# Gated linear attention: the short levels' differences kept, their products computed in one burst

## The chip, the cores and the metric

The kernel runs on one NeuronCore of one Trainium2 chip. The metric is the device time of one execution in microseconds (us), as the median of several runs; lower is better. The engines are called as the profile calls them: PE (TensorE), DVE (VectorE), ACT (ScalarE), POOL (GpSimd) and SP (SyncE, which issues most of the transfers).

## What is computed

One layer of a hybrid decoder, for a prompt of 512 tokens and 8 sample tokens. One combined projection feeds a dilated window attention and a gated linear attention (GLA) of 4 heads; then come an output merge, a projection and a feed-forward part. The change lies in the prompt's GLA alone, which the reference computes chunk by chunk:

```python
cum = jnp.cumsum(gc, axis=2)
diff = cum[:, :, :, None, :] - cum[:, :, None, :, :]
decay = jnp.exp(jnp.where(causal[None, None, :, :, None], diff, -jnp.inf))
scores = jnp.einsum('bhtsd,bhsd->bhts', qc[:, :, :, None, :] * decay, kc)
o = (jnp.einsum('bhts,bhsv->bhtv', scores, vc)
     + jnp.einsum('bhtd,bhdv->bhtv', qc * jnp.exp(cum), state))
```

So for each pair of tokens s <= t of a chunk the score is the sum over 128 features of q(t) k(s) exp(cum(t) - cum(s)).

## The kernel before, in words

The kernel holds activations with features on the 128 partitions and 520 tokens (512 of the prompt, 8 samples, in two halves of 260) along the free dimension. Every projection is a chain of panels: 128 output columns of a weight, loaded by SP, split by ACT (`whi`, L90) and DVE (`wlo`, L91) into two parts, and multiplied on PE in three passes by the halves of the activations (`panel_mms`, L124). A panel has 48 such matmuls of 128x260; the text calls them panel matmuls.

The attention and GLA parts are written as Python generators. `fill` advances one of them between panels, so that their small instructions are recorded among the panel matmuls. What is recorded is not yet the order: the framework's scheduler (a timeline model in the build) then orders each engine's instructions, within the dependencies, the priorities (`split_panel` has a high one) and the buffers of the pools.

GLA takes one head after another (`gla`), in chunks of 128 tokens, while the projections of the GLA inputs and of the two output gates (`gA`, `gB`) run. For one head: `zp` (the gate's matmul), its log-sigmoid on ACT and DVE, the running sum `cum` (L567), the operands `qe` and `kl` (multiplied on POOL, L574 and L579), and the transposes `klp` on PE (L582). Then come the scores, by levels. A pair of tokens whose common block has length 2L (first in the left half, second in the right half) belongs to level L; with a difference `D` of `cum` to the value at the middle of the block, the left half of `D` becomes k exp(-D/16) and the right half q exp(D/16), and one product gives all pairs of the level. LEVELS is (64, 32, 16, 8, 4, 2). Each level has one DVE subtraction (L609), two exponentials on ACT (L611, L612), two multiplications on DVE (L613, L614) and matmuls into a PSUM bank `lev`. Level 64 takes 4 matmuls of 64x64 (L617) and level 32 takes 8 of 32x32 (L622); DVE copies them into the score tile `ST` (L618, L626). The four short levels (16, 8, 4, 2) use `blocks` (L552): 16 matmuls, each of a 32-token block with itself, each into one quarter of the partitions. DVE merges each of them into `sd` under the mask of the level (`copy_predicated`, L630). Ahead of the levels stands a group for a token with itself and for neighbouring pairs (two calls of `blocks`, L601 and L602 merge them). POOL copies `sd` into `ST` (L633), and `ST` is an operand of the outputs `gpo` (L639).

Most matmuls use the array at its full width of 128 columns; `blocks`, level 32 and the sample's `gso` use 32 columns, level 64 uses 64. The text calls them narrow, and a stretch of narrow matmuls without a wide one between them a run.

Of the kernel before, what the change touches and what calls it, by code (L numbers as in the profile page):

```python
# [9 lines left out]
F32 = mybir.dt.float32  # L10
F32R = mybir.dt.float32r
U8 = mybir.dt.uint8
AF = mybir.ActivationFunctionType
ALU = mybir.AluOpType
# [3 lines left out]

D = 1024
S = 512  # L20
NB = 8
P = 128
# [5 lines left out]
LEVELS = (64, 32, 16, 8, 4, 2)  # L28
# [16 lines left out]
class Build:  # L45
# [175 lines left out]
    def stats(self, ap, xr):  # L221
# [14 lines left out]
        for j in range(2):  # L236
            self.rsqrt(ap, self.rb[:, j * HC:(j + 1) * HC], pr[:, j, :HC], HC, 1 / D)

# [316 lines left out]
    def gla(self, gp, h):  # L555
        nc = self.nc
        k, q = self.QKb[:, h, :S], self.QKb[:, 4 + h, :S]
# [2 lines left out]
        zp = self.bank("zp")  # L560
        nc.tensor.matmul(zp, wg, pv(halves(self.G)), start=True, stop=True)
        cum = gp.tile([P, S], F32, tag="cum", name="cum", bufs=1)
        D = gp.tile([P, S], F32, tag="D", name="D", bufs=3)
        self.logsig(gp, D, zp, S)
        for c in range(4):
            cc = slice(c * P, (c + 1) * P)
            nc.vector.tensor_tensor_scan(cum[:, cc], self.ones, D[:, cc], 0.0, op0=ALU.mult, op1=ALU.add)  # L567
        yield
# [8 lines left out]
                                op=ALU.subtract)  # L577
# [9 lines left out]
        sd = gp.tile([P, 4, 32], F32, tag="sd", name="sd", bufs=1)  # L587
# [3 lines left out]
        lm = lambda n: self.c["lmask"][:, n].unsqueeze(1).to_broadcast([P, 4, 32])  # L591

        vw = lambda t, L: t.rearrange("p (n x l) -> p n x l", x=2, l=L)
        D = gp.tile([P, S], F32, tag="D", name="D", bufs=3)[:, :256]
        nc.vector.tensor_tensor(D, cum[:, 1::2], cum[:, 0::2], op=ALU.subtract)
        nc.scalar.activation(D, D, AF.Exp, scale=1 / 16)
        nc.vector.tensor_tensor(D, D, q[:, 1::2], op=ALU.mult)
        ps = self.bank("lev")[:, :192].rearrange("p (c t) -> p c t", c=4)
        self.blocks(ps[:, :, :32], k, q, 32)
        self.blocks(ps[:, :, 32:], k, D, 16)  # L600
        nc.vector.copy_predicated(sd, lm(0), ps[:, :, :32])  # L601
        nc.vector.copy_predicated(sd[:, :, 1::2], lm(1)[:, :, 1::2], ps[:, :, 32:])  # L602
        yield
        for li, L in enumerate(LEVELS):
            ps = self.bank("lev")
            n = S // (2 * L)
            D = gp.tile([P, S], F32, tag="D", name="D", bufs=3)
            Dv, kv, qv = (vw(t, L) for t in (D, k, q))
            nc.vector.tensor_tensor(D.rearrange("p (n l) -> p n l", n=n), cum.rearrange("p (n l) -> p n l", n=n),  # L609
                                    vw(cum, L)[:, :, 0, L - 1:L].to_broadcast([P, n, 2 * L]), op=ALU.subtract)  # L610
            nc.scalar.activation(Dv[:, :, 0], Dv[:, :, 0], AF.Exp, scale=-1 / 16)  # L611
            nc.scalar.activation(Dv[:, :, 1], Dv[:, :, 1], AF.Exp, scale=1 / 16)  # L612
            nc.vector.tensor_tensor(Dv[:, :, 0], Dv[:, :, 0], kv[:, :, 0], op=ALU.mult)  # L613
            nc.vector.tensor_tensor(Dv[:, :, 1], Dv[:, :, 1], qv[:, :, 1], op=ALU.mult)  # L614
            if L == 64:
                for c in range(4):
                    nc.tensor.matmul(ps[:64, c * 64:(c + 1) * 64], Dv[:, c, 0], Dv[:, c, 1], start=True, stop=True)  # L617
                nc.vector.tensor_copy(ST[:64, :, 64:], ps[:64, :256].rearrange("p (c t) -> p c t", c=4))  # L618
            elif L == 32:
                for c in range(4):  # L620
                    for x in range(0, P, 64):
                        nc.tensor.matmul(ps[x:x + 32, c * 32:(c + 1) * 32], Dv[:, 2 * c + x // 64, 0],  # L622
                                         Dv[:, 2 * c + x // 64, 1], start=True, stop=True)
                for x in range(0, P, 64):
                    rows = slice(x, x + 32)
                    nc.vector.tensor_copy(ST[rows, :, x + 32:x + 64], ps[rows, :P].rearrange("p (c t) -> p c t", c=4))  # L626
            else:
                psv = ps[:, :P].rearrange("p (c t) -> p c t", c=4)
                self.blocks(psv, D, D, 32)
                nc.vector.copy_predicated(sd, lm(li), psv)  # L630
            yield
        for x in range(0, P, 32):
            nc.gpsimd.tensor_copy(ST[x:x + 32, :, x:x + 32], sd[x:x + 32])  # L633
        st = None
# [2 lines left out]
        for c in range(4):  # L637
            po = self.bank("gpo")
            nc.tensor.matmul(po[:, :256], ST[:, c], V[:, c], start=True, stop=(c == 0))  # L639
            if c:  # L640
                nc.tensor.matmul(po[:, :256], qe[:, c * P:(c + 1) * P], st, start=False, stop=True)  # L641
            pu = self.bank("gpu")
            nc.tensor.matmul(pu[:, :256], klT[:, c * P:(c + 1) * P], V[:, c], start=True, stop=True)  # L643
            sn = gp.tile([P, 256], F32, tag="state", name="state", bufs=2)
            if c:
                nc.vector.scalar_tensor_tensor(sn, st, el[:, c:c + 1], pu[:, :256], op0=ALU.mult, op1=ALU.add)
            else:
                nc.vector.tensor_copy(sn, pu[:, :256])
            st = sn
            nc.scalar.activation(os[:, c], po[:, :256], AF.Copy)  # L650
            jk = gp.tile([P, S], F32, tag="D", name="jk", bufs=3)
            nc.scalar.activation(jk[:, :256], po[:, :256], AF.Square, accum_out=ssq[:, c:c + 1])
            yield
        nc.gpsimd.dma_start(self.O["pgla"][h], st)
# [494 lines left out]
```

## Time and profile before

| what | value |
|---|---|
| median of 3 runs | 945.26 us (945.14 to 946.29) |
| the profiled execution | 943.87 us |
| its span, first to last instruction | 942.1 us |
| mean granted TensorE clock | 0.993 |

The profile is one execution. The time around its span is 1.8 us, and the execution lies 1.4 us under the median. In a row of the timeline stand the start, the busy time, the engine, the line, the operation with output and inputs, the size and a count; a bracket at the end tells how long the engine had been idle and what ended that. Starts of consecutive matmuls, not their busy times, tell what a matmul costs, since matmuls are pipelined. An fp32 matmul leaves two records, one of a panel or a transpose leaves one; so 16 matmuls of `blocks` are 32 records.

### The profile page before, as it was taken

The numbers are of one execution on the slowest core, as the hardware profiler recorded it, in microseconds if no ns is written. First come the engines' busy times: TensorE is split into PE (matmuls) and PEld (weight loads), VectorE is DVE, ScalarE is ACT, GpSimd is POOL, SyncE is SP. The second block draws the span as 40 slices with busy tenths as digits, with TensorE's granted clock in tenths as the row PEclk, the third lists the DMA queues.
The fourth block names the chain that finished last, engine by engine and source line by source line (L and its number), as shares of the span: only waits on it lengthen the run. The fifth ranks groups of instructions, "written<-read, shape, count | busy, mean of one in ns | idle before, by whom it ended". The sixth has DMA issues, their size and how long they took to land.

```text
span 942.1 us, 19815 instructions
## 1 busy us (share of the span) xinstructions
PE 921.9 (98%) x8290; PEld 902.7 (96%) x8290; DVE 550.0 (58%) x1079; ACT 376.7 (40%) x732; POOL 72.4 (8%) x125
## 2 busy tenths in 40 slices
PE   6999999999999999999999999999999999999995
PEld 6999999999988998999999999999999999999995
DVE  6756746844775958676755556433443344555664
ACT  5232233362544545564733444422432243224432
POOL 4000001000201112010000000000000000000000
PEclk9999999998999999999999999999999999999998
DMA  6366545311545344222677766777775222323301
GB/s 226 126 219 223 187 145 204 113 68 47 160 165 200 114 163 143 83 73 70 230 269 268 269 246 247 269 275 275 276 270 179 90 91 89 100 102 98 128 25 67
DMA packets 37579, 155.27 MB, mean 165 GB/s; under 512 B 5177, under 2 KB 11585, under 8 KB 35538
## 3 DMA queue, kind: packets, MB, share of 16 engines
q1 hardware_dynamic: 32498, 95.26, 29.6%
q0 software_dynamic: 4848, 58.73, 17.9%
q8 instruction: 65, 1.06, 0.5%
q14 instruction: 24, 0.20, 0.1%
q10 hardware_dynamic: 144, 0.01, 0.0%
HBM read 140.66 MB, written 54.17 MB: 207 GB/s over the span
## 4 chain that ended last, share of the span: by engine, by line
PE 96%; DVE 2%; issue 1%; ACT 1%; DMA 0%; SPq 0%; DVEq 0%; ACTq 0%
PE mps L124 80%; PE mps L981 5%; PE pvp L365 1%; PE lev L552 1%; PE ptp L354 1%; PE gpo L639 1%; PE gpu L643 1%; PE vps L305 1%; PE gso L706 1%; PE gpo L641 1%; PE spO L151 1%; PE sps L339 1%; DMA raw<-in_w_in 0%; PE mps L516 0%; PE sps L334 0%
## 5 line engine op out<-in xcount | busy, mean ns | idle before, releaser
L90 ACT ACTIVATE whi<-raw 128x512 fp32r<-128x512 f32 x264 | 165.8, 630 | 372.6 <-PE mps L124 329.8
L91 DVE TENSOR_TENSOR wlo<-raw,whi 128x512 fp32r<-128x512 f32 x264 | 182.4, 692 | 148.3 <-ACT whi L90 145.9
L124 PE MATMUL mps<-uh,whi 128*128 128x260 f32 x928 | 195.3, 290 | 6.6 <-ACT whi L90 5.3
L124 PE MATMUL mps<-ul,whi 128*128 128x260 f32 x928 | 194.5, 289 | 1.9 <-DVE ul L215 1.9
L124 PE MATMUL mps<-uh,wlo 128*128 128x260 f32 x928 | 193.8, 288 | 0.0
L124 PEld LDWEIGHTS mps<-uh,whi 128*128 128x128 f32 x928 | 145.8, 191 | 9.4 <-ACT whi L90 6.4
L124 PEld LDWEIGHTS mps<-ul,whi 128*128 128x128 f32 x928 | 145.6, 191 | 5.1 <-DVE ul L215 2.5
L124 PEld LDWEIGHTS mps<-uh,wlo 128*128 128x128 f32 x928 | 146.3, 191 | 1.3 <-issue 0.6
L124 PE MATMUL mps<-hh,whi 128*128 128x260 f32 x512 | 103.2, 283 | 0.0
L124 PE MATMUL mps<-hh,wlo 128*128 128x260 f32 x512 | 103.2, 283 | 0.0
L124 PE MATMUL mps<-hl,whi 128*128 128x260 f32 x512 | 103.0, 283 | 0.0
L124 PEld LDWEIGHTS mps<-hh,whi 128*128 128x128 f32 x512 | 79.0, 188 | 0.1
L124 PEld LDWEIGHTS mps<-hh,wlo 128*128 128x128 f32 x512 | 78.9, 188 | 0.0
L124 PEld LDWEIGHTS mps<-hl,whi 128*128 128x128 f32 x512 | 78.7, 188 | 0.0
L124 PE MATMUL mps<-fh,wlo 128*128 128x260 f32 x384 | 77.3, 283 | 0.0
L124 PE MATMUL mps<-fl,whi 128*128 128x260 f32 x384 | 77.2, 283 | 0.0
L124 PE MATMUL mps<-fh,whi 128*128 128x260 f32 x384 | 76.8, 282 | 0.0
L124 PEld LDWEIGHTS mps<-fh,wlo 128*128 128x128 f32 x384 | 59.2, 188 | 0.0
L124 PEld LDWEIGHTS mps<-fl,whi 128*128 128x128 f32 x384 | 59.0, 188 | 0.0
L124 PEld LDWEIGHTS mps<-fh,whi 128*128 128x128 f32 x384 | 59.0, 188 | 0.0
L981 PE MATMUL mps<-fh,lw 128*128 128x260 f32 x256 | 46.6, 283 | 0.0
L981 PEld LDWEIGHTS mps<-fh,lw 128*128 128x128 f32 x256 | 39.6, 188 | 0.1
(334 smaller groups left out, 1312.8 us busy)
## 6 DMA issues: line engine op xcount, KB each, us to landing
raw<-in_w_in SPq DMA_DIRECT2D x57, 512.0 KB, 3.5
raw<-in_w_up SPq DMA_DIRECT2D x32, 512.0 KB, 4.8
raw<-in_w_down SPq DMA_DIRECT2D x32, 512.0 KB, 4.8
sx<-in_state SPq DMA_DIRECT2D x8, 512.0 KB, 4.3
sx<-dV SPq DMA_DIRECT2D x8, 512.0 KB, 4.7
out_sgla<-sx POOLq DMA_DIRECT2D x8, 512.0 KB, 5.4
raw<-in_w_pb SPq DMA_DIRECT2D x8, 512.0 KB, 5.8
raw<-in_w_o SPq DMA_DIRECT2D x8, 512.0 KB, 5.7
```

Source lines behind the costliest of these rows:

```text
L90: nc.scalar.activation(hi, raw[:, x:x + n], AF.Copy)
L91: nc.vector.tensor_tensor(lo, raw[:, x:x + n], hi.bitcast(F32), op=ALU.subtract)
L124: self.last = nc.tensor.matmul(out[j], w, x[:, k, j * HC:(j + 1) * HC], start=(k == 0 and n == 0), stop=(k == kt - 1 and n == 2))
L151: self.nc.tensor.matmul(*args, **kw)
L305: nc.tensor.transpose(pt[:, r * P:(r + 1) * P], vt[:, r * P:(r + 1) * P], self.c["ident"])
L339: nc.tensor.matmul(pss[hh][:, hp, gg * P:(gg + 1) * P], Q[rows, i, b * P:(b + 1) * P], K[rows, i, b * P:(b + 1) * P], start=True, stop=True)
L354: nc.tensor.transpose(pt[:, hh, x], prs[hp][:, hh, x * P:(x + 1) * P], self.c["ident"])
L365: nc.tensor.matmul(po[:, hh * 64:hh * 64 + 64], prT[:, hh, x], v, start=(x == first), stop=(x == 1))
L552: self.nc.tensor.matmul(ps[32 * i:32 * i + 32, c], k[:, 32 * b:32 * b + 32], q[:, n * b:n * b + n], start=True, stop=True)
L639: nc.tensor.matmul(po[:, :256], ST[:, c], V[:, c], start=True, stop=(c == 0))
L641: nc.tensor.matmul(po[:, :256], qe[:, c * P:(c + 1) * P], st, start=False, stop=True)
L981: nc.tensor.matmul(ps, w, x[:, kk, cc], start=(kk == 0 and n == 0), stop=(kk == KT - 1 and n == 2))
```

## The change

The pair group keeps its difference in a tile of its own (`Dp`) and is no longer multiplied at once. The levels 64 and 32 go on as before. Each short level makes its operand `D` and keeps it; the tag `D` has four buffers instead of three. When all four are there, one stretch of code multiplies everything: the two calls of `blocks` of the pair group into one PSUM bank, and the four short levels side by side into a second (`lev4`). Six merges into `sd` follow.

```diff
-        D = gp.tile([P, S], F32, tag="D", name="D", bufs=3)[:, :256]
...
-        ps = self.bank("lev")[:, :192].rearrange("p (c t) -> p c t", c=4)
-        self.blocks(ps[:, :, :32], k, q, 32)
-        self.blocks(ps[:, :, 32:], k, D, 16)
-        nc.vector.copy_predicated(sd, lm(0), ps[:, :, :32])
-        nc.vector.copy_predicated(sd[:, :, 1::2], lm(1)[:, :, 1::2], ps[:, :, 32:])
+        Dp = gp.tile([P, S // 2], F32, tag="Dp", name="Dp", bufs=1)
+        nc.vector.tensor_tensor(Dp, cum[:, 1::2], cum[:, 0::2], op=ALU.subtract)
+        nc.scalar.activation(Dp, Dp, AF.Exp, scale=1 / 16)
+        nc.vector.tensor_tensor(Dp, Dp, q[:, 1::2], op=ALU.mult)
         yield
-        for li, L in enumerate(LEVELS):
-            ps = self.bank("lev")
+        short = []
+        for L in LEVELS:
             n = S // (2 * L)
-            D = gp.tile([P, S], F32, tag="D", name="D", bufs=3)
+            D = gp.tile([P, S], F32, tag="D", name="D", bufs=4)
...
             else:
-                psv = ps[:, :P].rearrange("p (c t) -> p c t", c=4)
-                self.blocks(psv, D, D, 32)
-                nc.vector.copy_predicated(sd, lm(li), psv)
+                short.append(D)
             yield
+        ps = self.bank("lev")[:, :192].rearrange("p (c t) -> p c t", c=4)
+        psl = self.bank("lev4").rearrange("p (l c t) -> p l c t", l=4, c=4)
+        self.blocks(ps[:, :, :32], k, q, 32)
+        self.blocks(ps[:, :, 32:], k, Dp, 16)
+        for li, D in enumerate(short):
+            self.blocks(psl[:, li], D, D, 32)
+        nc.vector.copy_predicated(sd, lm(0), ps[:, :, :32])
+        nc.vector.copy_predicated(sd[:, :, 1::2], lm(1)[:, :, 1::2], ps[:, :, 32:])
+        for li in range(4):
+            nc.vector.copy_predicated(sd, lm(2 + li), psl[:, li])
+        yield
```

In the changed kernel the lines behind the loop's start are other ones: the subtraction L609 is L604, the multiplications L613 and L614 are L608 and L609, the matmuls of level 64 are L613 and of level 32 L619, their copies L614 and L623, the merges L633, L634 and L636. The scheduler orders everything around it anew, so the built programs differ in more than these lines. Three places show it.

First, PE in the first head, from the transposes `klp` on. Before, the pair group (operands `QKb` and `D`) follows at once, and each level has its own place:

```order
L582 MATMUL klp_2881<-ident_185,kl_2877 128x128 x4
L552 MATMUL lev_2960<-QKb_2502 32x32 x16
L552 MATMUL lev_2960<-D_2956,QKb_2502 32x16 x16
L706 MATMUL gso_2888<-sx_2630,qz_2637 32x256 x4
L617 MATMUL lev_3008<-D_3009 64x64 x4
...
L622 MATMUL lev_3091<-D_3092 32x32 x8
...
L552 MATMUL lev_3121<-D_3122 32x32 x16
...
L552 MATMUL lev_3222<-D_3223 32x32 x16
...
L552 MATMUL lev_3246<-D_3247 32x32 x16
L552 MATMUL lev_3270<-D_3271 32x32 x16
```

In the changed program of the same place the names are the same, with `Dp` for the pair group's operand and `lev4` for the second bank:

```order
L582 MATMUL klp_2881<-ident_185,kl_2877 128x128 x4
L712 MATMUL gso_2888<-sx_2630,qz_2637 32x256 x8
...
L613 MATMUL lev_2979<-D_2973 64x64 x4
...
L619 MATMUL lev_3062<-D_3056 32x32 x8
...
L305 MATMUL vps_3162<-ident_185,vt_3159 128x128 x4
L552 MATMUL lev_3187<-QKb_2502 32x32 x16
L552 MATMUL lev_3187<-Dp_2956,QKb_2502 32x16 x16
L552 MATMUL lev4_3188<-D_3086 32x32 x16
L552 MATMUL lev4_3188<-D_3169 32x32 x16
L552 MATMUL lev4_3188<-D_3175 32x32 x16
L552 MATMUL lev4_3188<-D_3181 32x32 x16
```

All six calls of `blocks` now stand in one run behind transposes of another tile, 59 panel matmuls after `klp`; between the left-out rows stand panel matmuls.

Second, PE in the last head, again from `klp` on. Before:

```order
L582 MATMUL klp_5065<-ident_185,kl_5061 128x128 x4
L552 MATMUL lev_5140<-QKb_2502 32x32 x16
L552 MATMUL lev_5140<-D_5136,QKb_2502 32x16 x16
L617 MATMUL lev_5175<-D_5176 64x64 x4
L622 MATMUL lev_5187<-D_5188 32x32 x8
...
L552 MATMUL lev_5204<-D_5205 32x32 x16
L552 MATMUL lev_5289<-D_5290 32x32 x16
L552 MATMUL lev_5313<-D_5314 32x32 x16
...
L552 MATMUL lev_5337<-D_5338 32x32 x16
```

And in the changed program, the same engine and place:

```order
L582 MATMUL klp_5116<-ident_185,kl_5112 128x128 x4
...
L613 MATMUL lev_5198<-D_5192 64x64 x4
L619 MATMUL lev_5210<-D_5204 32x32 x8
L552 MATMUL lev_5305<-QKb_2502 32x32 x16
L552 MATMUL lev_5305<-Dp_5127,QKb_2502 32x16 x16
L552 MATMUL lev4_5306<-D_5221 32x32 x16
L552 MATMUL lev4_5306<-D_5227 32x32 x16
...
L552 MATMUL lev4_5306<-D_5293 32x32 x16
L552 MATMUL lev4_5306<-D_5299 32x32 x16
```

Here the scheduler splits the burst: levels 16 and 8 come with levels 64 and 32 (20 panel matmuls after `klp`, where before the first narrow matmul follows at once), and levels 4 and 2 come 32 panel matmuls later. From `zp` to `klp` stand 90 panel matmuls, before 79. The third head is split in the same way (25 panel matmuls between the pieces), the first and the second have one burst. Counted over all four heads and the samples, PE has 24 runs of narrow matmuls before and 18 now (17 and 10 with levels in them, 7 and 8 of `gso` alone), and inside runs it changes between 32 and 64 columns 4 times before and 2 times now.

Third, DVE in the last head, from the operand `kl` on. Before, two levels are subtracted ahead (`D_5176`, `D_5188`), and each further subtraction follows a merge or a copy:

```order
L576 TENSOR_TENSOR kl_5061<-cum_5045 128x512
L595 TENSOR_TENSOR D_5136<-cum_5045 128x256
L609 TENSOR_TENSOR D_5176<-cum_5045 128x512
L609 TENSOR_TENSOR D_5188<-cum_5045 128x512
...
L601 COPY_PREDICATED sd_5132<-lmask_197,lev_5140 128x128
L609 TENSOR_TENSOR D_5205<-cum_5045 128x512
L602 COPY_PREDICATED sd_5132<-lmask_197,lev_5140 128x64
L618 COPY ST_5134<-lev_5175 64x4x64
L609 TENSOR_TENSOR D_5290<-cum_5045 128x512
L626 COPY ST_5134<-lev_5187 32x4x32 x2
L609 TENSOR_TENSOR D_5314<-cum_5045 128x512
```

In the changed program four levels are subtracted ahead, and levels 4 and 2 (`D_5293`, `D_5299`) follow the copies out of levels 64 and 32:

```order
L576 TENSOR_TENSOR kl_5112<-cum_5096 128x512
L595 TENSOR_TENSOR Dp_5127<-cum_5096 128x256
L604 TENSOR_TENSOR D_5192<-cum_5096 128x512
L604 TENSOR_TENSOR D_5204<-cum_5096 128x512
L604 TENSOR_TENSOR D_5221<-cum_5096 128x512
L604 TENSOR_TENSOR D_5227<-cum_5096 128x512
...
L614 COPY ST_5125<-lev_5198 64x4x64
L604 TENSOR_TENSOR D_5293<-cum_5096 128x512
L623 COPY ST_5125<-lev_5210 32x4x32 x2
L604 TENSOR_TENSOR D_5299<-cum_5096 128x512
L633 COPY_PREDICATED sd_5123<-lmask_197,lev_5305 128x128
L608 TENSOR_TENSOR D_5293<-D_5293,QKb_2502 128x64x4
```

Since the four buffers are taken by levels 64 to 8, level 4 can be subtracted only when PE has read level 64 out of its buffer, and level 2 when PE has read level 32.

More of the change, by code (lines that the diff above doesn't have):

```diff
@@ L593, in gla @@
         vw = lambda t, L: t.rearrange("p (n x l) -> p n x l", x=2, l=L)
-        D = gp.tile([P, S], F32, tag="D", name="D", bufs=3)[:, :256]
-        nc.vector.tensor_tensor(D, cum[:, 1::2], cum[:, 0::2], op=ALU.subtract)
-        nc.scalar.activation(D, D, AF.Exp, scale=1 / 16)
-        nc.vector.tensor_tensor(D, D, q[:, 1::2], op=ALU.mult)
-        ps = self.bank("lev")[:, :192].rearrange("p (c t) -> p c t", c=4)
-        self.blocks(ps[:, :, :32], k, q, 32)
-        self.blocks(ps[:, :, 32:], k, D, 16)
-        nc.vector.copy_predicated(sd, lm(0), ps[:, :, :32])
-        nc.vector.copy_predicated(sd[:, :, 1::2], lm(1)[:, :, 1::2], ps[:, :, 32:])
+        Dp = gp.tile([P, S // 2], F32, tag="Dp", name="Dp", bufs=1)
+        nc.vector.tensor_tensor(Dp, cum[:, 1::2], cum[:, 0::2], op=ALU.subtract)
+        nc.scalar.activation(Dp, Dp, AF.Exp, scale=1 / 16)
+        nc.vector.tensor_tensor(Dp, Dp, q[:, 1::2], op=ALU.mult)
         yield
-        for li, L in enumerate(LEVELS):
-            ps = self.bank("lev")
+        short = []
+        for L in LEVELS:
             n = S // (2 * L)
-            D = gp.tile([P, S], F32, tag="D", name="D", bufs=3)
+            D = gp.tile([P, S], F32, tag="D", name="D", bufs=4)
             Dv, kv, qv = (vw(t, L) for t in (D, k, q))
@@ L615, in gla @@
             if L == 64:
+                ps = self.bank("lev")
                 for c in range(4):
@@ L619, in gla @@
             elif L == 32:
+                ps = self.bank("lev")
                 for c in range(4):
@@ L650, in gla @@
             nc.scalar.activation(os[:, c], po[:, :256], AF.Copy)
-            jk = gp.tile([P, S], F32, tag="D", name="jk", bufs=3)
+            jk = gp.tile([P, S], F32, tag="D", name="jk", bufs=4)
             nc.scalar.activation(jk[:, :256], po[:, :256], AF.Square, accum_out=ssq[:, c:c + 1])
```

## The prediction

> **What bounds the kernel now.** I read the page's busy times first, then the stretches by stage, then PE's waits in the stage of the change, and last the timeline there.
>
> ```profile
> PE 921.9 (98%) x8290; PEld 902.7 (96%) x8290; DVE 550.0 (58%) x1079; ACT 376.7 (40%) x732; POOL 72.4 (8%) x125
> core 0: us, PE busy (x) PEld busy (x) DVE busy (x) ACT busy (x) POOL busy (x), PEclk, DMA share, GB/s
> 245.00:462.00 217.00, 215.07 (x2461) 202.31 (x2460) 155.50 (x373) 119.33 (x264) 28.89 (x41) 1.00 0.40 131
> 462.00:566.00 104.00, 104.00 (x869) 104.00 (x868) 61.88 (x97) 40.68 (x64) 7.83 (x16) 1.00 0.74 266
> PE lev L617 <- DVE D L614: 0.8, 1, 0.8
> PE klp L582 <- POOL kl L579: 0.6, 1, 0.6
> PE gso L706 <- PE lev L552: 0.5, 1, 0.5
> ```
>
> PE is the bound nearly everywhere. The GLA stage runs from 245 to 462 us of the span; there PE is busy for 215.07 of 217.00 us at a granted clock of 1.00, and the three rows of waits make up the 1.9 us that are missing. The stage behind it (462 to 566) has PE busy without a gap. So what PE saves in GLA, in work or in waits, should reach the end undiminished, and what DVE (155.50 of 217) or ACT save is worth nothing unless PE waits for it. The change removes no matmul, no merge and no exponential. Two things are left to count: what narrow runs cost PE beyond their matmuls, and PE's waits.
>
> **What a run costs.** The timeline of PE in the first head has a single call of `blocks` between panel matmuls, and two calls in one run:
>
> ```profile
> 268.09 0.40 PE L124 MATMUL mps<-uh,wlo 128*128 128x260 f32 x2
> 268.33 0.40 PE L124 MATMUL mps<-uh,whi 128*128 128x260 f32 x2
> 268.66 0.46 PE L552 MATMUL lev<-D 128*32 128x32 f32 x32
> 269.05 0.52 PE L124 MATMUL mps<-ul,whi 128*128 128x260 f32 x2
> 269.40 0.41 PE L124 MATMUL mps<-uh,wlo 128*128 128x260 f32 x2
> ...
> 271.33 0.40 PE L124 MATMUL mps<-ul,whi 128*128 128x260 f32 x2
> 271.66 0.76 PE L552 MATMUL lev<-D 128*32 128x32 f32 x64
> 272.35 0.51 PE L124 MATMUL mps<-uh,wlo 128*128 128x260 f32 x2
> 272.69 0.40 PE L124 MATMUL mps<-uh,whi 128*128 128x260 f32 x2
> ```
>
> Two panel matmuls take 0.24 us (268.09 to 268.33), one 0.12. From 268.33 to 269.40 stand four of them and one call: 1.07 - 0.48 = 0.59 us for the call. From 271.33 to 272.69 stand four and two calls: 1.36 - 0.48 = 0.88 us. So a call costs 0.29 us, and entering and leaving a run costs 0.30 us once. Beside transposes it is less:
>
> ```profile
> 315.86 0.60 PE L582 MATMUL klp<-ident,kl 128*128 128x128 f32 x4
> 316.39 0.46 PE L552 MATMUL lev<-QKb 128*32 128x32 f32 x32
> 316.67 0.48 PE L552 MATMUL lev<-D,QKb 128*32 128x16 f32 x32
> 317.07 0.68 PE L617 MATMUL lev<-D 128*64 128x64 f32 x8
> ...
> 295.80 0.60 PE L305 MATMUL vps<-ident,vt 128*128 128x128 f32 x4
> 296.24 0.60 PE L663 MATMUL gop<-ident,os 128*128 128x128 f32 x4
> ```
>
> Four transposes take 0.44 us (295.80 to 296.24); from `klp` to the first narrow matmul pass 0.53, so entering costs 0.09. From 316.67 to 317.07 pass 0.40 where a call takes 0.28 (316.39 to 316.67), so going from 32 to 64 columns inside a run costs 0.12, about as much as leaving. A run between transposes therefore costs about 0.2.
>
> **Term 1, fewer runs.** The order has 24 runs before and 18 now. Six runs at 0.30 are 1.8 us, at 0.2 they are 1.2; of the changes of width inside runs, 4 before and 2 now, two at 0.12 are gone, 0.2 us. The ends are 1.2 and 2.0. Many of the runs that vanish stood beside transposes (`klp`, `gsp`, `vps`), so I take 1.5 us, nearer the low end.
>
> [...]
>
> **Term 2, the three waits of before.** Each is tied to its place in PE's order:
>
> ```profile
> 324.69 0.64 PE L706 MATMUL gso<-sx,qz 128*32 128x256 f32 x8 [0.53 <-PE lev L552]
> 422.49 0.66 PE L582 MATMUL klp<-ident,kl 128*128 128x128 f32 x4 [0.59 <-POOL kl L579]
> 424.62 0.65 PE L617 MATMUL lev<-D 128*64 128x64 f32 x8 [0.79 <-DVE D L614]
> ...
> 324.43 0.16 DVE L693 TENSOR_TENSOR qz<-kqs,as__3831 128x8 f32<-128x8 f32 x1
> ...
> 420.82 1.61 POOL L579 TENSOR_TENSOR kl<-kl,QKb 128x512 f32<-128x512 f32 x1 [16.95 <-ACT kl L578]
> 422.40 1.47 POOL L574 TENSOR_TENSOR qe<-qe,QKb 128x512 f32<-128x512 f32 x1
> ...
> 421.22 1.50 DVE L597 TENSOR_TENSOR D<-D,QKb 128x256 f32<-128x256 f32 x1
> 422.64 1.50 DVE L613 TENSOR_TENSOR D<-D,QKb 128x256 f32<-128x256 f32 x1
> 424.07 0.41 DVE L614 TENSOR_TENSOR D<-D,QKb 128x256 f32<-128x256 f32 x1
> ```
>
> `klp` in the last head waits 0.59 us for POOL's `kl`. The chain from `zp` to `kl` keeps its instructions on DVE, ACT and POOL, but 90 panel matmuls instead of 79 stand between `zp` and `klp`, 11 x 0.12 = 1.3 us more cover. That wait should go. Level 64 then waited 0.79 us for its product L614, which ended at 424.48. Now 20 panel matmuls (2.4 us) stand between, and the two calls (0.6 us) no longer do: 1.8 us later. Two more subtractions (0.6 us each, from 426.94 to 427.54 below) stand ahead of its product on DVE, but those products sat out POOL's two multiplications anyway (1.50 instead of 0.41), so they mostly fill that hole. That wait goes too, with some 1 us to spare. The 0.53 us ahead of `gso` in the second head is put down to `lev`, which had long been done; DVE's `qz` ended at 324.59, 0.1 us before. Now 69 panel matmuls stand between `klp` and that `gso` instead of 41: 3.4 us later, against two subtractions (1.2 us) more on DVE. All three are 1.9 us; at worst they stay (0).
>
> **Term 3, new waits.** Levels 4 and 2 are subtracted only when PE has read levels 64 and 32 from their buffers, so a chain on DVE stands between level 64's matmuls and the burst's last calls. Its prices, from the last head:
>
> ```profile
> 426.61 0.41 DVE L618 COPY ST<-lev 64x256 f32<-64x256 f32 x1
> 426.94 0.67 DVE L609 TENSOR_TENSOR D<-cum 128x512 f32<-128x512 f32 x1
> 427.54 0.57 DVE L626 COPY ST<-lev 32x128 f32<-32x128 f32 x2
> 428.13 0.69 DVE L609 TENSOR_TENSOR D<-cum 128x512 f32<-128x512 f32 x1
> ...
> 429.19 0.70 DVE L762 TENSOR_TENSOR gB<-mps,rb 128x520 f32<-128x520 f32 x1
> ...
> 431.08 0.41 DVE L614 TENSOR_TENSOR D<-D,QKb 128x256 f32<-128x256 f32 x1
> 431.41 0.41 DVE L613 TENSOR_TENSOR D<-D,QKb 128x256 f32<-128x256 f32 x1
> ...
> 432.69 0.28 DVE L630 COPY_PREDICATED sd<-lmask,lev 128x128 f32<-128x128 uint8 x1
> ```
>
> By starts: the copy 0.33, two subtractions 1.2, two copies 0.6, two merges 0.5, four products at 0.33 (431.08 to 431.41) 1.3: 3.9 us. With one or two panel instructions (`wlo` or `gB`, 0.6 each) that come ahead it is 4.5 to 5.1. PE's cover in the last head is level 32 and four calls (about 1.5), 32 panel matmuls (3.8) and one call (0.3): 5.6 us. In the third head it is 25 panel matmuls, 4.8 us. In the first, from level 32 on, 31 panel matmuls, four transposes and five calls (3.7 + 0.4 + 1.5) stand against a chain that starts at level 32. So the cover is thin, and an instruction or two may be late: I take 0.7 us in all (one panel instruction of 0.6 too many). The ends are 0, and 1.3 us in each head, 5.2.
>
> Two things cost nothing. The merges now all come after the last call; then POOL copies `sd` and `gpo` follows, 61 panel matmuls (7.3 us) later in the last head, which hides four merges (1.1), two panel instructions and the copies. And only SBUF pays for the fourth buffer; no DMA, table load or queue of SP is moved past another that PE waits for, and the granted clock is at 1.00 in this stage already.
>
> **Sum.** -1.5 - 1.9 + 0.7 = -2.7 us, against the profiled execution's 943.87 (span 942.1): 941.2. The median of the runs shown is 945.26, 1.4 above that execution, so I forecast 942.6 for the median, with an own range of 941.4 to 943.3. A measurement of this kernel tells about 0.2%, 1.9 us, from no change; faster means below 943.4.
>
> **Rivals.** *No change to be measured.* The waits only move: term 1 holds and 1.9 us of waits come back at the split bursts, 945.26 - 1.5 = 943.8 us. For it: before, each of the waits came at a place that the scheduler had thought ready. Against it: the places of after have more cover. Chance 0.31.
>
> *Slower.* The chain of term 3 is late in every head. Against the forecast's -3.4 us without new waits, +1.9 is reached when new waits come to 5.3 us, 1.3 in each head, that is when two panel instructions more than counted stand ahead of the products in all four. Three of them (1.8 us a head, 7.3 in all) would give 945.26 - 3.4 + 7.3 = 949.2. For it: DVE is at 72% in this stage (155.50 of 217), and POOL's multiplications stretched products from 0.41 to 1.50; four subtractions now stand where two stood, so one more may be caught, 1.1 us. Against: PE stands 1 us clear at level 64, and DVE has the same work in all. Chance 0.11. [...]
>
> [...] Chance 0.13. It shares its sign with the forecast, which has 0.45.
>
> **How the numbers follow.** Faster is 0.45 + 0.13 = 0.58, the same 0.31, slower 0.11. The range leaves out what lies under 941.2 (0.05) and most of the slower case: up to 945.8, since a few waits more than in the second case still give that.
>
> **What would show it.** PE's waits in the stage should list no `klp`, no level 64 and no `gso`; instead at most one wait of about 0.7 us of `lev` for a product of level 4 or 2. A burst of six calls should take about 0.30 + 6 x 0.29 = 2.0 us between panel matmuls. The stretch of PE from `zp` of the first head to the first matmul of the output projections should be shorter by about 2.7 us, and everything behind it as long as before. I am wrong if waits of `lev` for DVE add up to 3 us or more, or if panel matmuls begin to wait for `wlo`.

## The result, and the profile after

| kernel | median of 6 runs | profiled execution | its span |
|---|---|---|---|
| before | 945.66 us (945.13 to 947.31) | 943.87 us | 942.1 us |
| changed | 954.54 us (951.76 to 955.74) | 951.76 us | 950.0 us |

The changed kernel is slower: its time is 1.0075 of that before (95% interval 1.0058 to 1.0092; the two medians by themselves give 1.0094). Forecast were 942.6 us and a range up to 945.8. The forecast was wrong in sign.

First the stage that the prediction spoke of, from PE's `zp` of the first head to the first matmul of the output projections. Rows of PE's timeline, before:

```profile
244.07 1.02 PE L561 MATMUL zp<-G,wg 128*128 128x512 f32 x2
455.92 0.64 PE L124 MATMUL mps<-oas,whi 128*128 128x260 f32 x4
```

After, with the stretch of the stage (as in the prediction) and PE's waits in it:

```profile
245.67 1.02 PE L561 MATMUL zp<-G,wg 128*128 128x512 f32 x2
463.83 0.64 PE L124 MATMUL mps<-oas,whi 128*128 128x260 f32 x4
...
245.00:462.00 217.00, 209.91 (x2403) 197.83 (x2402) 151.17 (x359) 113.81 (x260) 32.38 (x41) 0.98 0.36 121
...
PE lev L552 <- issue: 4.2, 1, 4.2
PE lev L552 <- DVE D L609: 2.5, 3, 2.0
PE klp L582 <- POOL kl L579: 0.4, 1, 0.4
```

The stage took 211.85 us before (455.92 - 244.07) and takes 218.16 now: 6.31 us more, where 2.7 less were forecast. The other 1.6 us of the two spans' difference lie ahead of it (`zp` starts at 245.67 instead of 244.07), where PE's order is the same; behind it both spans have 486.2 us, as forecast. The three waits of before (1.9 us) are gone as forecast, and of the new ones the largest has no engine behind it: "issue" means that PE waited for nothing that the profile knows. PE's timeline in the second head, where it stands:

```profile
338.38 0.46 PE L552 MATMUL lev<-QKb 128*32 128x32 f32 x32
338.65 0.45 PE L552 MATMUL lev<-Dp,QKb 128*32 128x16 f32 x30
...
338.96 0.96 PE L552 MATMUL lev<-D 128*32 128x32 f32 x88
344.08 0.75 PE L552 MATMUL lev<-D 128*32 128x32 f32 x38 [4.17 <-issue]
344.76 0.80 PE L124 MATMUL mps<-uh,wlo 128*128 128x260 f32 x2
345.37 0.64 PE L124 MATMUL mps<-uh,whi 128*128 128x260 f32 x2
...
347.50 0.41 PE L124 MATMUL mps<-uh,wlo 128*128 128x260 f32 x2
```

The first calls run at the price forecast (0.27 us from 338.38 to 338.65). Then PE stops for 4.17 us. What comes next is 38 records, six more than a call has: PE stopped in the middle of a call, three matmuls short of its end, where no semaphore stands. Behind the stop two panel matmuls take 0.43 us instead of 0.24, until 347.50: 12 of them in 2.74 us, 1.3 us more than 12 x 0.12. The stretches show why (columns as before; the clock is the number after the busy times):

```profile
338.00:340.00 2.00, 1.92 (x159) 1.63 (x157) 0.60 (x2) 0.60 (x1) 0.00 (x0) 1.00 0.93 327
340.00:344.00 4.00, 0.00 (x0) 0.00 (x0) 0.00 (x0) 0.00 (x0) 0.00 (x0) 1.00 0.83 316
344.00:347.60 3.60, 3.52 (x51) 3.46 (x51) 1.21 (x4) 0.00 (x0) 1.16 (x5) 0.53 0.03 11
347.60:355.00 7.40, 7.40 (x58) 7.19 (x57) 2.90 (x5) 2.01 (x5) 0.18 (x1) 1.00 0.21 71
```

From 340 to 344 us no engine did anything, while the DMA engines were 83 to 93% busy at over 310 GB/s; and when PE went on, its clock was 0.53.

The other wait, 2.00 us for DVE, is in the first head. Rows of PE, ACT and DVE there:

```profile
271.56 1.07 PE L552 MATMUL lev<-D 128*32 128x32 f32 x96
274.63 0.46 PE L552 MATMUL lev<-D 128*32 128x32 f32 x32 [2.00 <-DVE D L609]
...
272.55 0.63 ACT L90 ACTIVATE whi<-raw 128x512 fp32r<-128x512 f32 x1 [4.30 <-DMA raw<-in_w_in]
273.09 0.42 ACT L606 ACTIVATE D<-D 128x256 f32<-128x256 f32 x1
...
273.21 0.69 DVE L91 TENSOR_TENSOR wlo<-raw,whi 128x512 fp32r<-128x512 f32 x1 [1.65 <-ACT whi L90]
274.16 0.42 DVE L609 TENSOR_TENSOR D<-D,QKb 128x256 f32<-128x256 f32 x1
```

The split of a weight panel stood ahead of level 2 on both engines, and its weights came 4.30 us late: ACT waited, the exponentials of level 2 behind it (273.09) too, DVE waited for `whi`, and PE for the product. Here too the panel matmuls that follow are slow for a while, by 1.3 us (10 take 2.17 us from 275.90 to 278.07, two take 0.58 from 278.59 to 279.17).

### The profile page after: what moved, and what is told of

It is laid out like the page before. It is cut to its first block, busy times and chain, and to the rows that moved or that the text cites. A ratio compares the mean times of both kernels' runs of the same rounds, so it can differ in the third digit from the quotient of the medians.

```text
span 950.0 us, 19800 instructions
## 1 busy us (share of the span) xinstructions
PE 921.7 (97%) x8290; PEld 902.8 (95%) x8290; DVE 550.6 (58%) x1079; ACT 377.2 (40%) x732; POOL 75.8 (8%) x125
## 3 DMA queue, kind: packets, MB, share of 16 engines
q0 software_dynamic: 4848, 58.73, 17.8%
## 4 chain that ended last, share of the span: by engine, by line
PE 83%; DVE 6%; DMA 5%; issue 2%; ACT 1%; SPq 1%; POOL 0%; DVEq 0%; ACTq 0%
PE mps L124 70%; PE mps L987 5%; DMA raw<-in_w_in 2%; PE pvp L365 1%; DVE wlo L91 1%; DMA kcb<-dq 1%; PE gpo L645 1%; PE gpu L649 1%; DVE D L604 1%; PE ptp L354 1%; DMA QTt<-ro 1%; PE lev L552 1%; PE gpo L647 1%; DMA xr<-in_xT 1%; PE sps L339 1%
```

## What stops PE: a theory and its rivals

The page lists a queue that the prediction had passed over. Of the changed kernel:

```profile
PE 921.7 (97%) x8290; PEld 902.8 (95%) x8290; DVE 550.6 (58%) x1079; ACT 377.2 (40%) x732; POOL 75.8 (8%) x125
...
q8 instruction: 65, 1.06, 0.4%
```

65 packets of 16 KB are moved in a span in which PE issues 16,580 weight loads and matmuls: 255 of them per packet. In panel work, 17 instructions a microsecond, a packet lasts 15 us. A call of `blocks` is 64 instructions (16 matmuls in fp32, each two loads and two matmuls) in 0.29 us; six calls are 384 in about 1.8 us. *The fetch theory*, worked out from these numbers and tried in the runs below: PE gets its instructions in packets of 256, asked for one ahead; a long narrow run uses up a packet faster than the next one comes, all the more when the DMA engines are busy with other data. The packet in question, seen in the queues (packets, MB, share of the engines), in the first two rows from 338 to 341.8, in the last from 341.8 to 343 us:

```profile
q1 hardware_dynamic: 560, 0.66, 53.3%
q0 software_dynamic: 189, 0.70, 45.1%
...
q8 instruction: 1, 0.02, 5.0%
```

In the first 3.8 us queue q8 had none (a second instruction queue, q14, moved one packet of 8 KB); it began at 341.88, ended at 342.85, and PE went on at 344.08. The rivals: products that DVE delivers late; four levels in one PSUM bank; something in narrow matmuls themselves.

## The experiments

In the table, "stage" is the time from `zp` of the first head to the first output projection, as above, in one profiled execution; "stops" are PE's waits on issue in it, "products" its waits for DVE's operands of the levels.

| kernel | time against before | stage | stops | products |
|---|---|---|---|---|
| before | 1 | 211.85 | 0 | 0.8 |
| changed | 1.0075 (1.0058 to 1.0092) | 218.16 | 4.2 | 2.5 |
| shifted by 128 instructions | 1.0053 (1.0028 to 1.0077) | 216.46 | 2.3 + 1.9 | 0.5 |
| shifted by 192 | 1.0154 (1.0111 to 1.0197) | 218.60 | 5.1 + 1.6 + 0.3 + 0.2 | 0.3 |
| before, six calls more a head | 1.0219 (1.0172 to 1.0265) | 235.75 | 9.8 in four | 2.4 |
| five buffers | 1.0068 (1.0044 to 1.0093) | 219.45 | 4.9 | 0 |
| three calls and three | 1.0010 (0.9990 to 1.0029) | 214.79 | 1.8 + 0.2 | 1.4 |
| three, three, five buffers | 1.0007 (0.9983 to 1.0031) | 213.97 | 0 | 1.1 |
| pair group back | 1.0033 (1.0018 to 1.0048) | 213.57 | 1.4 + 0.3 | 1.6 |
| short levels first | 1.0039 (1.0016 to 1.0062) | 218.58 | 0 | 2.2 |
| short first, five buffers | 1.0004 (0.9982 to 1.0026) | 215.27 | 0 | 4.3 |
| changed, no state traffic | 0.9977 (0.9952 to 1.0003) | 211.24 | 2.4 | 0.9 |
| the same once more | 0.9979 (0.9959 to 1.0000) | 213.15 | 2.8 | 0.9 |
| before, no state traffic | 0.9981 (0.9959 to 1.0002) | 211.41 | 0 | 1.0 |

**The same order, shifted.** In the changed kernel, with 32 and with 48 matmuls more at the start:

```diff
         pr = self.ps.tile([P, 2, 512], F32, tag="rps", name="rps")
+        for _ in range(32):
+            nc.tensor.matmul(pr[:, 0, :2], self.ones, self.ones[:, :2], start=True, stop=True)
```

> The changed kernel with 32 matmuls of 2 columns more at its very start, while PE still waits for its first data: 128 more PE instructions, and behind them the same order of PE. Nothing of the result changes. The fetch theory (PE's instructions come in 16 KB packets of 256; a burst of six calls issues 384 in 1.8 us and stops when the next packet is not there yet; where it stops depends on where the packet ends fall): the border that fell on the start of the second head's burst now falls 128 instructions later in it, so 250 instead of nearly all of its instructions come behind the border. The stop of 4.2 us shrinks to between 0 and 1.2 us; in the first head a stop of about 2 us takes the place of the wait for DVE. Time 3 to 5 us under the changed kernel's, that is 3 to 6 us above before. The rivals (products late on DVE; one PSUM bank for four levels; the clock): the same PE order and the same DVE chain, so the stop of 4.2 us stays where it was, 7 to 9 us above before.

> As the run before with 48 matmuls, 192 PE instructions more. The fetch theory: the border falls some 70 instructions into the second head's burst and more than 300 follow, so a stop of about 4 us comes at the end of that burst, later in it than in the changed kernel; the first head keeps its wait for DVE. Time as the changed kernel's, 6 to 9 us above before, and 2 us or more above the run with 128. The rivals: no difference between 128 and 192, both as the changed kernel.

With 128 more, PE stops in the first head, in the middle of a call, and in the second head not in the burst any more but some 3.5 us behind it, between two panel matmuls of one and the same panel:

```profile
276.65 0.66 PE L554 MATMUL lev<-D 128*32 128x32 f32 x40 [2.26 <-issue]
...
344.68 0.41 PE L124 MATMUL mps<-uh,whi 128*128 128x260 f32 x2
346.96 0.39 PE L124 MATMUL mps<-ul,whi 128*128 128x260 f32 x1 [1.87 <-issue]
```

With 192, the stop stands at the end of the burst, 4 records before it:

```profile
344.70 1.24 PE L554 MATMUL lev<-D 128*32 128x32 f32 x122
351.02 0.32 PE L554 MATMUL lev<-D 128*32 128x32 f32 x4 [5.08 <-issue]
```

So the stop moved as the fetch theory said, and the rivals have no reason for that: from `zp` of the first head on, PE's order is the same in the two shifted kernels, and from the second head on it is that of the changed kernel too (in the first head levels 64 and 32 and some transposes stand in other places there, and the wait of 2.00 us is gone in both; with 192 it was expected to stay). The panel matmuls that stop have nothing else to wait for; by the theory, the burst ahead of them had used up what was there. How many instructions PE had issued when it stopped can be read from the stretches that begin at 0 (matmuls, then loads): of the changed kernel, of that with 128 (two stops), and with 192 (two):

```profile
0.00:342.00 342.00, 326.41 (x3006) 313.96 (x3007) 221.68 (x494) 137.75 (x302) 36.12 (x59) 0.99 0.47 158
...
0.00:275.40 275.40, 272.67 (x2372) 266.28 (x2373) 177.36 (x380) 106.06 (x223) 28.10 (x46) 0.99 0.47 158
0.00:346.50 346.50, 341.11 (x3136) 329.78 (x3136) 224.86 (x500) 138.36 (x303) 38.04 (x64) 0.99 0.47 158
...
0.00:348.00 348.00, 342.80 (x3136) 330.99 (x3137) 222.34 (x494) 137.90 (x302) 37.27 (x59) 1.00 0.46 155
0.00:445.00 445.00, 434.99 (x4153) 418.57 (x4154) 287.75 (x645) 188.06 (x409) 54.08 (x78) 0.99 0.42 141
```

6013, 4745, 6272, 6273 and 8307: over 256 these leave 125, 137, 128, 129 and 115. With PE's few other instructions, which the trace has but these columns leave out (56 to 78 up to there, counted from PE's first), every one leaves 193. The sizes were missed: the second head was to stop for 0 to 1.2 us with 128 and stopped 1.87, and the two stops together are as long as the one of before; what the stage gained, 1.7 us, it gained in waits for products. And the added matmuls cost time at the start, which the expectations had not counted: with 192, `zp` of the first head starts at 254.42, 8.8 us later than in the changed kernel, so the time of that run, 14.6 us over before where 6 to 9 were expected, tells little of the stops.

**A long run in the kernel before.**

```diff
                 nc.vector.copy_predicated(sd, lm(li), psv)
+            if li == 5:
+                psx = self.bank("levx").rearrange("p (l c t) -> p l c t", l=4, c=4)
+                for lx in range(6):
+                    self.blocks(psx[:, lx % 4], D, D, 32)
```

> The kernel before, and behind each head's last level six more calls of blocks on the same operand, into a bank that nobody reads: runs of 7 or 8 calls (448 or 512 PE instructions), with no change in buffers, products or merges that matter. By the matmuls alone (0.29 us a call): 24 x 0.29 = 7.0 us, 6.5 to 8 us above before, no stop within a run. The fetch theory: a stop within the run in all four heads, of 1.6 to 4.4 us each, so 14 to 21 us above before. The theory that only late DVE products stop the burst: 7 us, since these runs wait for nothing new.

PE's waits in the stage, the queue of instructions on its page, and the stretches from 0 to each of the four stops:

```profile
PE levx L552 <- issue: 9.8, 4, 4.8
q8 instruction: 71, 1.16, 0.5%
...
0.00:278.00 278.00, 263.93 (x2499) 255.46 (x2499) 177.39 (x384) 106.15 (x223) 28.80 (x51) 0.99 0.47 157
0.00:345.00 345.00, 327.63 (x3389) 314.99 (x3389) 221.18 (x496) 136.51 (x300) 37.40 (x64) 0.99 0.47 155
0.00:399.80 399.80, 377.94 (x4153) 362.02 (x4154) 258.23 (x590) 160.47 (x361) 46.90 (x74) 0.99 0.45 149
0.00:451.80 451.80, 426.27 (x4791) 407.87 (x4791) 289.43 (x656) 188.06 (x415) 50.85 (x80) 0.98 0.42 139
```

A stop in every head, though nothing of the change is in this kernel; 4998, 6778, 8307 and 9582 leave 134, 122, 115 and 110 over 256, and with the other instructions 193 again. The 24 added calls are 1,536 PE instructions, six times 256, and q8 has six packets more, 71 instead of 65: it is PE's queue. The stops are 2.31, 4.76, 2.27 and 0.50 us long; the last was to be at least 1.6. The time is 2.2% over before, some 20 us, where the matmuls alone are 7 and the stops 9.8; what is left goes with slow panel matmuls behind the stops (a granted clock of 0.55 in the 2.6 us behind the first) and some 1 us more of other waits, and was not added up. That a long narrow run stops without any of the change's kept operands, late products or merges is shown by this. The stretches from the run to the end of the stop, of the first and of the second head, give a hint of what sets the length:

```profile
275.00:279.40 4.40, 2.11 (x220) 1.99 (x219) 0.87 (x3) 0.00 (x0) 1.35 (x5) 1.00 0.01 4
341.70:348.30 6.60, 1.98 (x210) 1.87 (x210) 0.98 (x5) 0.00 (x0) 1.35 (x5) 0.97 0.83 299
```

With the DMA engines 1% busy the stop is 2.31 us, with them 83% busy 4.76.

**Five buffers** of `D` (`bufs=5` for 4; the sample's `vs` moves into the buffer of `ov`).

> The changed kernel with five buffers of D instead of four (the sample's vs shares the buffer of ov to make the space): level 4 is subtracted without waiting for PE, only level 2 waits, and for level 64 alone. The theory of late products: the 2.5 us of waits for DVE's L609 shrink to under 1 us, 1.5 to 2.5 us under the changed kernel's time. If late products were all of the loss, the time would come to that of before. The fetch theory: the second head's burst starts 8 instructions later against the packet borders, so its stop of about 4 us stays, and the bursts of five calls in the last two heads (320 instructions) may stop too: 5 to 9 us above before.

PE's waits in the stage:

```profile
PE lev L552 <- issue: 4.9, 1, 4.9
PE klp L582 <- POOL kl L579: 2.8, 2, 1.7
```

No wait for a product is left, the stop stays, at 6013 instructions as in the changed kernel, and the time is within that kernel's interval. The stop doesn't come from late products. What these cost by themselves this run can't tell: in the order that the scheduler made for five buffers, `klp` waits for POOL's `kl`, 2.8 us, and the stop is 0.7 us longer, so that the expected gain of 1.5 us had no way to show.

**The burst cut.** In the first kernel the pair group and level 16 go together, and 8, 4 and 2:

```diff
+            elif L == 16:
+                ps = self.bank("lev")[:, :320].rearrange("p (c t) -> p c t", c=4)
+                self.blocks(ps[:, :, :32], k, q, 32)
+                self.blocks(ps[:, :, 32:48], k, Dp, 16)
+                self.blocks(ps[:, :, 48:], D, D, 32)
...
-        self.blocks(ps[:, :, :32], k, q, 32)
-        self.blocks(ps[:, :, 32:], k, Dp, 16)
         for li, D in enumerate(short):
             self.blocks(psl[:, li], D, D, 32)
```

> The burst cut in two: the pair group and level 16 (three calls) are multiplied when level 16's operand is there, levels 8, 4 and 2 (three calls) at the end. Buffers as in the changed kernel. The fetch theory (a packet is asked for 64 instructions ahead of a border, and PE stops 320 instructions after that if it has not come, which takes 3.8 us, and up to 6.1 us while other transfers run): no stop in the first two heads, since no 320 instructions hold more than 240 narrow ones; in the last two the order still has 304 in one piece, so 0 to 1.4 us each. With 1.2 us less for runs and 1.9 us of waits gone, against 0 to 2.5 us of waits for products: between 3 us under and 2 us above before, 5 to 10 us under the changed kernel. If late products on DVE were the cause: these are as late as in the changed kernel, and the time stays 5 us or more above before.

> The run before with five buffers of D (vs in the buffer of ov, as in the other run with five). The waits for products go (under 0.5 us in all), but in the last two heads levels 64 and 32 and five calls stand in one run, 368 instructions. The fetch theory: no stop in the first two heads, one of 0 to 2 us in each of the last two: 3 us under to 2 us above before. If late products are all that costs, 2 to 3 us under before, with no stop anywhere.

In the third only the pair group goes back to its old place.

> One part of the change undone: the pair group is multiplied and merged at once again, as before; only the four short levels are kept and multiplied in one burst, side by side in one bank. The burst has 256 instructions in the first two heads, two pieces of 128 in the others. The fetch theory: it needs 280 or more in the wrong place for a stop without other transfers, 235 with them; so 0 to 1.2 us in each of the first two heads and none in the others, 1 us under to 3 us above before, 5 to 9 us under the changed kernel. If the shared bank or the four kept operands were the cause of the loss, the time stays 5 us or more above before.

All three are back at or near the time of before, the third just over the upper end of what was expected (3.1 us above, by the ratio, where 3 were allowed). The third has its four levels side by side in one bank as in the changed kernel, and loses less than half as much; so the bank can't be what most of the 7 us are lost by. The stops that are left are short and where the order still has some 300 narrow instructions in one piece, in the third head: 1.85 us with three and three (up to 1.4 was expected), 1.45 with the pair group back (none was expected, since levels 64 and 32, which join the run in the order, had been forgotten). Three and three with five buffers has no stop, and still is no faster than before: PE's waits in its stage come to 4.4 us (1.1 of them for products, where under 0.5 was expected, 1.1 for `kl`, the others for `gA`, `os` and `el`) against 1.9 before.

**Without the state traffic.** During the second head's burst the sample part moves its states: two loads of 512 KB to `sx` and a store per half head.

```diff
-                nc.sync.dma_start(st, I["state"][bs, h].rearrange("b d v -> d b v"))
-                nc.sync.dma_start(vb, dV[bs].unsqueeze(0).to_broadcast([P, 4, 256]))
+                if h == 0:
+                    nc.sync.dma_start(st, I["state"][bs, h].rearrange("b d v -> d b v"))
+                    nc.sync.dma_start(vb, dV[bs].unsqueeze(0).to_broadcast([P, 4, 256]))
...
-                nc.gpsimd.dma_start(O["sgla"][bs, h].rearrange("b d v -> d b v"), vb)
+                nc.gpsimd.dma_start(O["sgla"][bs, h].rearrange("b d v -> d b v")[:, :, :32], vb[:, :, :32])
```

> The changed kernel, with the transfers of the sample part cut: the sample states are loaded for the first head alone (the others compute on what is left in the tile), and of the updated states only an eighth is stored. PE's order is the same up to the second head's burst. The theory that the fetched packet is held up by other transfers: in the second head some 320 GB/s moved during the burst and the packet started 3.5 us after the burst's start; now there is little traffic, it starts within 2 us, and the stop shrinks from 4.2 to 2 to 2.6 us, at the same instruction. The theory that fetching takes this long by itself: the stop stays at 4 us or more. Late products or the shared bank: no stop that ends in the middle of a call, or no change to it.

> The kernel before with the same cut of the sample's transfers as in the changed kernel's run without state traffic (states loaded for the first head alone, an eighth of the updated ones stored), the fair partner of that run. The theory that fetched instructions and weights held up by this traffic are what the change loses by: before has no run that outpaces the fetch, so it gains little, 0 to 2 us under before; against it the changed kernel without the traffic stands within 2.5 us, instead of 7 to 9. If the traffic costs both kernels alike, this run gains 5 us or more, as the changed kernel did.

> The changed kernel without the state traffic once more, beside the kernel before without it: 943 to 947 us where before has 945 to 948; stop in the second head 2 to 2.6 us at the same instruction. By the fetch theory 0 to 2.5 us above its partner, by the theory that the traffic costs both alike 6 us or more above it.

PE in the first and the second head of the changed kernel without the traffic, and the queues of the 4 us from 332.4 on:

```profile
270.10 1.29 PE L552 MATMUL lev<-D 128*32 128x32 f32 x128
...
333.01 0.94 PE L552 MATMUL lev<-D 128*32 128x32 f32 x87
336.36 0.55 PE L552 MATMUL lev<-D 128*32 128x32 f32 x39 [2.41 <-issue]
337.18 0.40 PE L124 MATMUL mps<-uh,whi 128*128 128x260 f32 x2
337.42 0.40 PE L124 MATMUL mps<-ul,whi 128*128 128x260 f32 x2
...
q1 hardware_dynamic: 113, 0.40, 26.0%
q8 instruction: 1, 0.02, 1.6%
```

The stop, at 193 over 256 as before and one record earlier in the burst, is 2.41 us instead of 4.17 (2.80 in the other run, where at most 2.6 was expected). The packet began 1.7 us after the burst's first matmul (334.08 against 332.43) instead of 3.5 (341.88 against 338.38). Two panel matmuls behind it take 0.24 us at once (in the other run they slow to 0.43 for a while, from 1.6 us behind the stop's end on). In the first head the weights come in time and the wait of 2.00 us is gone: the last four calls run through in one row (270.10). That burst of six calls does not stop at all, in either run; the 0.9 us of products in the table stand in the last head. Against before, the changed kernel now stands at 0.9979 and its fair partner at 0.9981: the 0.75% are gone. Without the traffic the change makes no difference that can be measured, since the stop that is left (2.4 us) takes about what fewer runs (1.9, see below) and less of other waits (0.8) save; with it, it costs 7 us.

**Short levels first.** The loop runs over 16, 8, 4, 2, 64, 32, cut three and three, with four and with five buffers.

> The changed kernel with the levels in another sequence: 16, 8, 4 and 2 first, then 64 and 32; the pair group and level 16 are multiplied in one run of three calls, 8, 4 and 2 in another, as soon as they are there. The short levels then need no buffer that a long level holds, and the order has 3 runs in most heads. The fetch theory: no 320 instructions hold more than 240 narrow ones in the first three heads, no stop there, at most 0.5 us in the last; with 10 to 12 runs fewer than before at 0.2 to 0.3 us each and few waits for products: 2 to 5 us under before. If many narrow matmuls in a piece were slow for another reason (bank, clock), it stays 3 us or more above before.

> The run before with five buffers of D (vs in the buffer of ov). In the order levels 64 and 32 mostly join the second run, 240 instructions, and in the last head three runs of one to four calls. The fetch theory: no stop over 0.5 us in any head; 2 to 5 us under before. If waits for products are what remains, it is 1 us or more under the run with four buffers; else the two are alike within 1 us.

There is no stop in either, as expected, and no gain, against the expectation: 3.7 us over before with four buffers, which had been named as the sign of another reason (bank, clock), and level with before with five. The expectation had counted on 10 to 12 runs fewer; PE's rows have 20 and 18 runs, where before has 24. PE's waits in the stage come to 6.3 and 4.8 us, against 1.9 before. With four buffers, ACT has the sigmoid of `gA` (3.68 us) and its table load (1.28 us) ahead of the last head's `kl`, and POOL needs 3.61 us for it (1.61 before). PE, ACT and POOL there:

```profile
420.71 0.66 PE L582 MATMUL klp<-ident,kl 128*128 128x128 f32 x4 [2.81 <-POOL kl L579]
...
402.65 3.68 ACT L893 ACTIVATE gA<-gA 128x4160 f32<-128x4160 f32 x1
...
417.05 3.61 POOL L579 TENSOR_TENSOR kl<-kl,QKb 128x512 f32<-128x512 f32 x1 [18.76 <-ACT kl L578]
```

PE's panel matmuls behind that run slow again (two take 0.43 us instead of 0.24, 423.38 to 423.81). With five buffers PE waits 4.3 us for products in all. So what these two lose goes with waits that another order brings; that nothing else is in it was not shown. No version that beats the kernel before was found.

## Why the prediction was wrong, by its own steps

*Term 1, fewer runs (-1.5).* Right in sign, and the size is known only roughly. New waits are 7.1 us, slow panel matmuls 2.6 (twice 1.3), waits that went 1.9: 7.8 in sum, against 6.31 measured, so 1.5 us came off elsewhere; that is a remainder, and the same changed kernel without the traffic had stages 1.9 us apart in two executions. Taken run by run from PE's rows (from the start of the last wide matmul ahead to the first one behind, less waits and 0.12 us for the wide one), the 24 runs took 20.0 us before and the 18 take 19.1 now, 0.9 less, with the slow clock behind the stop in the later number; in the pair without state traffic it is 1.9 us (19.7 for 22 runs, 17.8 for 17).

*Term 2, the three waits (-1.9).* Right: none of them is in the list after. A `klp` of another head, the third, waits 0.38 instead.

*Term 3, late products (+0.7).* The mechanism was right, the size off: 2.5 us in three waits, 2.00 of them in the first head. One panel instruction did stand ahead of the product, as assumed; but it was priced at its own 0.6 us, and it was waiting for its weights, which came 4.30 us late. The step that failed is the sentence that no DMA moves past another that PE waits for: no DMA needs to move for a product to stand behind one.

*The step that decided:* "A burst of six calls should take about 0.30 + 6 x 0.29 = 2.0 us." The price per call was right, and where no stop fell in, so was the sum: in the first head without the state traffic the six calls took 1.83 us (269.49 to 271.32). In the second head they took 6.38 (338.38 to 344.76), since by the fetch theory they held more instructions than were delivered in that time. The longest narrow run of calls before was three (192 instructions), and no row of its trace showed a run stopping; the price was carried from 3 to 6 without asking what else six calls use up. The sum had no term for it. With it fell "the granted clock is at 1.00 in this stage already": it was 0.53 in the 3.6 us behind the stop. Stop and slow clock together are 4.2 + 1.3 in the second head alone, more than all that was to be won.

*The rivals.* "Slower" had the sign and put 0.11 on it, by DVE being late in every head. That is not what came: the waits for products are 2.5 us where it needed 5.3, and five buffers took them away and left the stop. That a rival had the right sign is luck. The rival with 0.13 (term 1 at its upper end of 2.0 us and no new wait) missed the sign with the forecast. The signs named for being wrong (3 us of waits for DVE, panel matmuls that wait for `wlo`) did not appear: 2.5 us and none. A trace that shows a wait on "issue" was not among them.

How much PE had at hand can be read from the changed kernel's trace: the packet ahead of the stop began at 325.94 us, when PE had begun 5,557 instructions, and up to the stop, at 6,081, q8 began no other. So PE went on for 524 instructions, about two packets, where the kernel before never has more than 324 between the starts of two packets. In panel work, at 17 instructions a microsecond, the next packet has 15 us to come, and the kernel before has no stop on issue in the stage; behind 384 instructions in 1.8 us PE stood for up to 5.08 us (shifted by 192).

*Left open.* How far ahead a packet is asked for was only inferred from where packets start (in the kernel before, from 500 us on, between 34 instructions ahead of the border at 193 over 256 and 16 behind it, 21 ahead in the median); the 64 instructions in the expectation of three calls and three, and what is worked out with them, are the author's estimate. In what way the state traffic delays the packet was not separated. And 1.6 us ahead of the stage, where the order is that of before, come and go between executions of all these kernels (`zp` of the first head starts between 243.7 and 250.5 us in the profiles that aren't shifted).

## What to carry to other kernels

Count instructions, not only their time: a run of these small matmuls issues some 200 a microsecond (384 in 1.83 us), and when it held more than about one fetched packet (256), it could stop here for the next one: runs of six calls and more mostly for 2.3 to 2.8 us with the DMA engines 1 to 40% busy, and for 4.2 to 5.1 us with them 68 to 97% busy. Whether it does hangs on where the packets' borders fall: the first head's six calls did not stop on issue in the changed kernel, and did, for 2.26 us, when the order was shifted by 128. Before gathering small work into one burst, compare its instructions with the longest such run that the trace already has; here no run of three calls (192) stopped by more than 0.2 us, and cutting the burst into three and three brought the time back to that of before. And when a wait on a product is priced, follow its queue to the transfer at its far end.

## What the runs showed of the hardware that was not expected

- PE's stops on issue fell at one place in every kernel: 193 over 256 in PE's count of instructions, in all 13 stops over 1 us of eight kernels, inside a call or between panel matmuls. In the changed kernel PE went on 1.2 us after a packet of q8 had ended (342.85 and 344.08), without the state traffic about 1.3 us (335.1 and 336.36).
- For runs of six calls and more, a stop inside the run lasted 2.3 to 2.8 us where the DMA engines were 1 to 40% busy from the run's start to the stop's end (five stops), and 4.2 to 5.1 us where they were 68 to 97% busy (four). Left out is the stop of 0.50 us in the last head of the kernel with six calls more: the 288 instructions ahead of it took 2.4 us, those ahead of the nine others 1.4 to 1.5.
- Behind most stops and waits of 1.8 us and more the granted clock fell, to a mean of 0.50 to 0.76 over the next 3 us or so, and panel matmuls took up to 0.22 instead of 0.12 us each; behind a stop of 2.41 us it did not.
